# A two-matrix MLP by seven products: the sums of w_ff2 from DMA to VectorE, differences to GpSimd, and a last LayerNorm shared out

## The chip, the cores and the metric

One Trainium2 chip, one of its cores. The metric is the device time of one execution in microseconds (us), the median of several; smaller is better. Engines: PE is TensorE, DVE is VectorE, ACT is ScalarE, POOL is GpSimd, SP is SyncE (here it only issues DMAs).

## The reference

One layer of a hybrid encoder on 1024 frames of width 1024 (16 learned tokens are put in front and dropped at the end). The part that matters here is its second half:

```python
h  = layer_norm(ALPHA * h + mix, ln_mix_g, ln_mix_b)      # mix = concat(...) @ w_out
ff = square(relu(h @ w_ff1)) @ w_ff2                      # 1024 -> 4096 -> 1024
h  = layer_norm(ALPHA * h + ff, ln_ff_g, ln_ff_b)
```

All of it is float32.

## The kernel before

A float32 operand is split into a high part (a cast on ACT, line 128) and a low part (what is left, a subtraction on DVE, line 129); a product is three matmuls: high by high, high by low, low by high. `part` does this for an operand of 128x1024 and puts it into one of five `ring` slots (tile `hl`); a slot comes free when the product that read it has ended.

The first 560 us (LayerNorm, input projection, convolutions, attention, most of the output projection) are the same in both kernels. Then come:

- **The last projection tiles.** `mix_tile` (line 727) makes one 128-row tile of the residual stream `acc`; its LayerNorm has small statistics steps on GpSimd (lines 738 to 747 and `rsqrt`, lines 91 and 93) and two 128x1024 passes on DVE (lines 122 and 124). The tiles come in the order 6, 7, 4, 5, 0, 1, 2, 3.
- **x1**, the normalised stream turned by the TensorE (`x1_block`: four 128x128 transposes into PSUM, split into high and low). The MLP's two matrix products are done by Strassen and Winograd's seven products in place of eight, over 2x2 blocks, so sums and differences of blocks are needed as well: `xb21`, `xb11`, `xb22` are blocks, `xt2`, `xt3`, `xt4`, `xt1` are turned differences of them, made in `x1_t2`, `second_half` and `third_half` with `vsum` (line 811, DVE).
- **Eight groups** (`group(g)`, g = 0 to 7), each for 512 of the 4096 hidden columns. `first_product` makes seven products of 24 matmuls of 512 columns for h @ w_ff1 (line 885), with squared ReLU behind them (`relu2`, lines 906 to 908, tiles `relu`). Then `group` makes seven products for w_ff2 (line 894), each added into `acc` by `add_to` (line 1008). Group 0 makes x1 as it goes; the others load x1 back from DRAM.

The seven right operands made of w_ff2's 2x2 blocks (256x512 each, 128x1024 in SBUF, 512 KB) are, in the order of the products, b11, t3 = b22 + b12, t2 = t3 + b11, t3 again with b11 and b21 added (called T4 in the change), b11 + b12, b21 and b22. In the kernel before these sums are made **by DMA**: `w2_load` (SP's queue, line 990) puts a block into a tile and `w2_add` (GpSimd's queue, line 997) adds another block to it from DRAM while it lands. Six such additions run per group, on GpSimd's queue in the order t3, t2, t2, b11, t3, t3. The last two wait until the first form of t3 has been split, and each waits for the one before:

```python
b_, a_ = part(t3, 2), part(a21, 2)     # line 1070
w2_add(t3, g, 0, 0)                    # line 1071
w2_add(t3, g, 1, 0)                    # line 1072
...
b, a = part(t3, 2), part(a22, 2)       # line 1088, fourth product
```

Each engine does its instructions in program order, and the order on each is set by a scheduler when the kernel is built; an instruction that waits holds all behind it on the same engine. Each DMA queue is issued in order too.

**The end.** `finish_rows(t)` is the last LayerNorm of tile t: mean on DVE (line 1032), sum of squares on ACT (1035), (a - mean) times gain on DVE with the gain in PSUM (1036), rsqrt on GpSimd. For t >= 4 ACT then scales (1042), a GpSimd DMA adds the bias row (1043) and SP stores (1044); for t < 4 two DVE passes do it (1047), and SP or ACT's queue stores (1050, 1052). In the last group tiles 4 to 7 are finished before tile 0's last products.

## Time and profile before

| what | value |
|---|---|
| time, three runs | 1268.98, 1258.01, 1263.7 us; median 1263.7 |
| the profiled execution's own time | 1269.01 us |
| its span, first to last instruction | 1267.2 us (1.8 us lie outside) |
| mean granted TensorE clock | 0.968 of full speed |
| busy share of the span | PE 92%, PE weight load 78%, DVE 75%, ACT 44%, POOL 11% |
| the eight groups with the last LayerNorm | from about 585 us to the end |

Busy shares are means over stages. What ends last in a stage is read from the idle time ahead of an instruction and what released it, which stands in square brackets behind a row of the timeline.

### The profile page before, as it was taken

What the parts mean: (1) busy time and instruction counts of PE and PEld (TensorE: products, weight loads), DVE (VectorE), ACT (ScalarE), POOL (GpSimd) and SP (SyncE); (2) the same over time, 40 slices, a digit from 0 to 9 for tenths busy, and PEclk for the clock granted to TensorE, in tenths of its full rate; (3) what the DMA queues carried; (4) which work ended last, traced back from release to release, by engine and by line L of the source; (5) the groups of instructions that cost most, each with busy time, mean ns of one, the idle gap of its engine ahead of it and who ended that gap; (6) DMA issues with size and microseconds to landing.
All of it is one profiled execution on the core that took longest, in us unless ns stands there. A gap on an engine that the chain in (4) does not pass through costs nothing.

```text
span 1267.2 us, 15601 instructions
## 1 busy us (share of the span) xinstructions
PE 1163.5 (92%) x5982; PEld 992.7 (78%) x5982; DVE 949.6 (75%) x1179; ACT 560.5 (44%) x951; POOL 143.4 (11%) x259
## 2 busy tenths in 40 slices
PE   5999996899899798997999989999999999998993
PEld 5999995789798677885778878788788787886882
DVE  6799977978788699779678575684765946658477
ACT  4522115666566445433643423434334352343544
POOL 3300002010000100142110010010100101001003
PEclk9999997999999899998999989999999998999997
DMA  9313111021111612206966757657776676765436
GB/s 291 120 41 88 55 51 51 17 51 34 26 26 51 199 34 67 84 17 236 279 210 193 257 136 233 184 127 269 202 237 192 149 258 192 222 205 121 150 83 199
DMA packets 72458, 178.58 MB, mean 141 GB/s; under 512 B 3849, under 2 KB 27696, under 8 KB 68288
## 3 DMA queue, kind: packets, MB, share of 16 engines
q1 hardware_dynamic: 54528, 140.32, 30.9%
q0 software_dynamic: 15936, 31.46, 14.8%
q10 hardware_dynamic: 1920, 5.81, 1.3%
q8 instruction: 47, 0.77, 0.3%
q14 instruction: 27, 0.22, 0.1%
HBM read 152.41 MB, written 18.87 MB: 135 GB/s over the span
## 4 chain that ended last, share of the span: by engine, by line
PE 44%; DVE 14%; DMA 12%; issue 7%; ACT 5%; POOL 1%; DVEq 0%; ACTq 0%; POOLq 0%
PE ps_g L885 15%; PE ps_g L894 13%; DMA t<-in_w_ff_dram 11%; PE ps_g L210 6%; PE ps_g L630 4%; DVE keepp L463 3%; DVE hl L129 2%; PE ps_t L513 2%; DVE relu L906 1%; PE ps_g L455 1%; DMA y_raw<-yscr 1%; PE ps_o L486 1%; DVE beta L465 1%; PE ps_o L489 1%; ACT hl L128 1%
## 5 line engine op out<-in xcount | busy, mean ns | idle before, releaser
L894 PE MATMUL ps_g<-hl 128*128 128x512 f32 x1344 | 323.7, 401 | 19.7 <-ACT hl L128 15.3
L894 PEld LDWEIGHTS ps_g<-hl 128*128 128x128 f32 x1344 | 258.3, 194 | 83.9 <-ACT hl L128 22.7
L210 PE MATMUL ps_g<-xh,w_hl 128*128 128x346 f32 (+4 forms) x1024 | 258.7, 332 | 0.9 <-ACT beta L460 0.9
L210 PEld LDWEIGHTS ps_g<-xh,w_hl 128*128 128x128 f32 x1024 | 179.9, 192 | 9.6 <-ACT beta L460 1.1
L210 PE MATMUL ps_g<-xl,w_hl 128*128 128x346 f32 (+4 forms) x512 | 169.8, 332 | 0.8 <-DVE xl L129 0.8
L1008 DVE TENSOR_TENSOR acc<-acc,ps_g 128x1024 f32<-128x1024 f32 x96 | 116.3, 1215 | 28.1 <-PE ps_g L894 28.1
L885 PE MATMUL ps_g<-x_T,hl 128*128 128x512 f32 x576 | 133.5, 390 | 0.7 <-DVE hl L129 0.4
L885 PEld LDWEIGHTS ps_g<-x_T,hl 128*128 128x128 f32 x576 | 107.6, 188 | 24.4 <-DVE hl L129 0.8
L210 PEld LDWEIGHTS ps_g<-xl,w_hl 128*128 128x128 f32 x512 | 98.2, 192 | 5.0 <-DVE xl L129 1.1
L463 DVE TENSOR_TENSOR_SCAN keepp<-keepp 128x912 f32<-128x912 f32 (+7 forms) x64 | 87.6, 1380 | 11.9 <-ACT keepp L459 11.4
L885 PE MATMUL ps_g<-x_Y,hl 128*128 128x512 f32 x384 | 90.5, 390 | 1.8 <-ACT x_Y L128 1.2
L128 ACT CAST hl<-w_raw 128x1024 fp32r<-128x1024 f32 x55 | 56.1, 1049 | 76.5 <-DVE w_raw L811 76.5
L885 PEld LDWEIGHTS ps_g<-x_Y,hl 128*128 128x128 f32 x384 | 71.8, 188 | 17.7 <-ACT x_Y L128 1.5
L885 PE MATMUL ps_g<-x_X,hl 128*128 128x512 f32 x360 | 84.3, 389 | 0.0
L128 ACT CAST hl<-relu 128x1024 fp32r<-128x1024 f32 x48 | 50.4, 1050 | 74.8 <-PE ps_g L894 41.7
L129 DVE TENSOR_TENSOR hl<-w_raw,hl 128x1024 fp32r<-128x1024 f32 x55 | 65.7, 1220 | 23.5 <-ACT hl L128 23.5
L285 DVE SCALAR_TENSOR_TENSOR cacc<-glu,prm,cacc 128x482 f32<-128x482 f32 (+3 forms) x120 | 82.7, 743 | 0.3
L885 PEld LDWEIGHTS ps_g<-x_X,hl 128*128 128x128 f32 x360 | 67.5, 188 | 14.0
L455 PE MATMUL ps_g<-ks,q_hl 128*128 128x456 f32 (+8 forms) x224 | 59.0, 366 | 10.8 <-ACT beta L460 3.9
L906 DVE TENSOR_TENSOR relu<-ps_g,relu 128x1024 f32<-128x1024 f32 (+1 forms) x27 | 29.8, 1104 | 51.5 <-PE ps_g L885 51.5
L459 ACT ACTIVATE keepp<-ps_g 128x456 f32<-128x456 f32 (+8 forms) x112 | 51.9, 468 | 33.9 <-PE ps_g L455 16.1
L630 PE MATMUL ps_g<-w_hl,y 128*128 128x512 f32 x240 | 63.8, 402 | 1.9 <-DVE w_hl L129 1.8
(210 smaller groups left out, 1763.0 us busy)
## 6 DMA issues: line engine op xcount, KB each, us to landing
x_X<-xscr SPq DMA_DIRECT2D x14, 2048.0 KB, 7.8
x_Y<-xscr SPq DMA_DIRECT2D x14, 2048.0 KB, 10.4
w_raw<-in_w_ff_dram SPq DMA_DIRECT2D x16, 1024.0 KB, 10.4
t<-in_w_ff_dram POOLq DMA_DIRECT2D x24, 512.0 KB, 6.6
w<-in_w_ff_dram SPq DMA_DIRECT2D x24, 512.0 KB, 5.7
raw<-in_w_in_dram SPq DMA_DIRECT2D x22, 512.0 KB, 4.2
w<-in_w_ff_dram POOLq DMA_DIRECT2D x16, 512.0 KB, 5.9
xt<-in_x_dram SPq DMA_DIRECT2D x8, 512.0 KB, 5.8
```

Source lines behind the costliest of these rows:

```text
L128: nc.scalar.copy(out=h, in_=src)
L129: nc.vector.tensor_tensor(out=l, in0=src, in1=f32(h), op=ALU.subtract)
L210: nc.tensor.matmul(dst[:, :cw], lhsT=w[:, a, k, :], rhs=b[:, k, c0:c0 + cw], start=(i == 0), stop=(i == 3 * KT - 1))
L285: nc.vector.scalar_tensor_tensor(out=acc, in0=glu[j][:, o + k:o + k + n], scalar=prm[:, j, k:k + 1], in1=acc, op0=ALU.mult, op1=ALU.add)
L455: nc.tensor.matmul(zp[:, :cm], lhsT=qs[h][:, m, i * P:(i + 1) * P], rhs=ks[:, h, c0:c0 + cm], start=(m == 0), stop=(m == 1 and not last))
L459: nc.scalar.activation(out=kp[h][:, c0:c0 + cw], in_=zp[:, :cw], func=AF.Sigmoid, scale=-0.125)
L463: nc.vector.tensor_tensor_scan(out=rev, data0=rev, data1=rev, initial=1.0, op0=ALU.mult, op1=ALU.bypass)
L630: nc.tensor.matmul(dst, lhsT=y[a][:, t * P:(t + 1) * P], rhs=w[b][:, n * 512:(n + 1) * 512], start=(i == 0), stop=(i == last))
L885: nc.tensor.matmul(bk, lhsT=a[:, u, k, j * P:(j + 1) * P], rhs=x[:, v, k, :], start=(start and i == 0), stop=(i == 11), skip_group_check=True)
L894: nc.tensor.matmul(prs[tt // 2][:, tt % 2], lhsT=a[:, x, u, tt * P:(tt + 1) * P], rhs=b[:, y, u, :], start=(start and i == 0), stop=(i == ...
L906: nc.vector.tensor_tensor(out=r[:, j], in0=bk, in1=r[:, j], op=ALU.add)
L1008: nc.vector.tensor_tensor(out=a, in0=a, in1=prs[h], op=op)
```

## The change

- `group(g)` loads the four blocks b11, b21, b22, b12 of w_ff2 as four plain loads on SP's queue at its start, ahead of the first seven products. After the second product's operands DVE makes three sums of 128x1024: t3 = b22 + b12, t2 = t3 + b11, T4 = t2 + b21 (signs are kept in the left operands). One addition by DMA is left per group, b12 to b11 (line 998 of the changed kernel). b21 and b22 are loaded again for the last two products as before.
- In the last products of a group the difference a21 - a12 is made ahead of the fifth product instead of ahead of the seventh.
- In group 0, ten of twelve 128x512 differences for x1 (all but tile 3's, and all four in `third_half`) and three sums of w_ff1 blocks (128x1024) go from DVE to GpSimd (`gsum`).
- The first eight blocks of x1 (`x1_first`, four tiles) stand in the code ahead of the last projection tiles, and all four `x1_t2` in `second_half`.
- The first piece of w_ff1 (`early_part(0)`) is asked for ahead of the groups.
- Last LayerNorm: tiles 6 and 7 have (a - mean) times rsqrt on ACT, times gain on GpSimd, bias by GpSimd's DMA; tile 0 takes the way of tiles 4 and 5 (ACT, then the DMA for the bias).

```diff
+    def gsum(dst, a, b, op):
+        nc.gpsimd.tensor_tensor(out=dst, in0=a, in1=b, op=op)
+
     def x1_t2(t):
         x, y = acc[:, t], acc[:, 4 + t]
-        vsum(diffs[:, 0, t], x[:, HALF[1]], x[:, HALF[0]], ALU.subtract)
-        vsum(diffs[:, 1, t], diffs[:, 0, t], y[:, HALF[0]], ALU.add)
+        fsum = vsum if t == order[7] else gsum
+        fsum(diffs[:, 0, t], x[:, HALF[1]], x[:, HALF[0]], ALU.subtract)
+        fsum(diffs[:, 1, t], diffs[:, 0, t], y[:, HALF[0]], ALU.add)
         x1_block(xt2, diffs[:, 1, t], cols_of(t), True)
 
-    done = 0
+    for i in range(4):
+        x1_first(i)
     for i in range(FIRST, 8):
         run(mix_tiles(i, i + 1))
-        while done < min(4 + i - FIRST, 2 * (i - FIRST + 1)):
...
             relu2(c11, pa, 1.0)
-            vsum(a11, a11, a21, ALU.add)
+            gsum(a11, a11, a21, ALU.add)
             b = part(a11, 4)
-            vsum(a11, a11, a22, ALU.add)
+            gsum(a11, a11, a22, ALU.add)
             a = part(a11, 4)
             xt3 = second_half()
+            yield
             product1(a, xt2, pa, False)
             keep_sum(c21, pa)
-            vsum(a21, a21, a22, ALU.add)
+            gsum(a21, a21, a22, ALU.add)
...
+        if t >= 6:
+            rsqrt(rs[:, 0:1], sm[:, 2:3], P, 1, 1.0 / D, LN_EPS)
+            nc.gpsimd.tensor_tensor(out=rs[:, 1:2], in0=mean, in1=rs[:, 0:1], op=ALU.mult)
+            nc.scalar.activation(out=y, in_=a, func=AF.Identity, scale=rs[:, 0:1], bias=rs[:, 1:2])
+            nc.gpsimd.tensor_tensor(out=a, in0=y, in1=rows[0], op=ALU.mult)
+        else:
...
+        if t == 0 or t >= 4:
+            if t < 6:
+                nc.scalar.activation(out=a, in_=y, func=AF.Copy, scale=rs[:, 0:1])
+            nc.gpsimd.dma_start(out=a, in_=rows[1], accum_op=ALU.add)
+            nc.sync.dma_start(out=out_rows, in_=a)
             return
...
     def group(g):
         first, last = g == 0, g == NG - 1
+        b11, b21 = (raw_tile(n).rearrange("p (u c) -> p u c", u=2) for n in ("b11", "b21"))
+        b12, b22 = w2_tile(), w2_tile()
+        for t, (r, c) in ((b11, (0, 0)), (b21, (1, 0)), (b22, (1, 1)), (b12, (0, 1))):
+            w2_load(t, g, r, c)
         steps = first_product(g)
+        next(steps)
+        vsum(b22, b22, b12, ALU.add)
+        vsum(b12, b22, b11, ALU.add)
+        vsum(b21, b12, b21, ALU.add)
+        t3, t2, t4 = b22, b12, b21
         r0, r1 = next(steps)
-        b11, t3 = (raw_tile(n).rearrange("p (u c) -> p u c", u=2) for n in ("b11", "t3"))
-        t2 = w2_tile()
-        for t, (r, c) in ((t3, (1, 1)), (b11, (0, 0)), (t2, (1, 1))):
-            w2_load(t, g, r, c)
-        w2_add(t3, g, 0, 1)
-        w2_add(t2, g, 0, 1)
-        w2_add(t2, g, 0, 0)
...
         b_, a_ = part(t3, 2), part(a21, 2)
-        w2_add(t3, g, 0, 0)
-        w2_add(t3, g, 1, 0)
...
-        b, a = part(t3, 2), part(a22, 2)
+        b, a = part(t4, 2), part(a22, 2)
         product(a, b, pb, False)
         add_to(1, 0, pb, False, sums)
         b21, b22 = (w2_load(w2_tile(), g, 1, c) for c in range(2))
         b, a = part(b11, 2), part(a11, 2)
+        vsum(a21, a21, a12, ALU.subtract)
         product(a, b, pa, False)
...
-        vsum(a12, a21, a12, ALU.subtract)
...
             d = diffs[:, 1, t]
-            vsum(d, d, acc[:, 4 + t, HALF[1]], ALU.subtract)
+            gsum(d, d, acc[:, 4 + t, HALF[1]], ALU.subtract)
```

The order on DVE at the turn from group 2 to group 3, in the kernel before. `w_7340` is group 2's last block of w_ff2, `relu_6967` holds the left operand of its last product, `w_raw` is group 3's piece of w_ff1, `acc` rows are the additions of products.

```order
L1008 TENSOR_TENSOR acc<-acc,ps_g 128x2x512 x2
L129 TENSOR_TENSOR hl<-relu_6967,hl 128x1024
L129 TENSOR_TENSOR hl<-w_7340,hl 128x1024
L1008 TENSOR_TENSOR acc<-acc,ps_g 128x2x512
L811 TENSOR_TENSOR relu_6967<-relu_6968,relu_6967 128x2x512
L1008 TENSOR_TENSOR acc<-acc,ps_g 128x2x512
L129 TENSOR_TENSOR hl<-relu_6967,hl 128x1024
L1008 TENSOR_TENSOR acc<-acc,ps_g 128x2x512
L129 TENSOR_TENSOR hl<-w_raw,hl 128x1024
```

The same place in the changed kernel. `w_7443` and `w_7444` are group 3's blocks b12 and b22, in the buffers from which group 2's last two blocks (`w_7338`, `w_7340`) were split just before; `b_7441` is its b11, `b_7442` its b21.

```order
L129 TENSOR_TENSOR hl<-relu_6975,hl 128x1024
L129 TENSOR_TENSOR hl<-w_7340,hl 128x1024
L1009 TENSOR_TENSOR acc<-acc,ps_g 128x2x512 x2
L811 TENSOR_TENSOR w_7444<-w_7444,w_7443 128x1024
L129 TENSOR_TENSOR hl<-relu_6976,hl 128x1024
L129 TENSOR_TENSOR hl<-w_raw,hl 128x1024
L811 TENSOR_TENSOR w_7443<-w_7444,b_7441 128x1024
L1009 TENSOR_TENSOR acc<-acc,ps_g 128x2x512
L811 TENSOR_TENSOR w_raw<-w_raw 128x4x256
L1009 TENSOR_TENSOR acc<-acc,ps_g 128x2x512
L811 TENSOR_TENSOR b_7442<-w_7443,b_7442 128x1024
L811 TENSOR_TENSOR w_raw<-w_raw 128x4x256
```

The first sum of group 3's w_ff2 blocks now stands ahead of the split of group 2's last left operand (`relu_6976`), the other two among group 2's last additions; the difference of left operands has gone from here to an earlier place.

The order on GpSimd at the last two projection tiles (2 and 3), in the kernel before. `mv` and `rs` are their means and inverse deviations, `rms` a factor of the projection, `t_6212` a tile of w_ff2's sums.

```order
L997 DMA t_6212<-in_w_ff_dram 128x2x512
L91 TENSOR_SCALAR ve<-ssum_5626 128x2
L91 TENSOR_SCALAR ve<-rs 128x1
L93 TENSOR_TENSOR rms<-ve,mhalf 128x2
L93 TENSOR_TENSOR rs<-ve,mhalf 128x1
L738 TENSOR_TENSOR mv<-sm_5711 128x1
```

The same place in the changed kernel, from tile 2's mean to its inverse deviation. `x_T_5640` holds the differences, `w_raw` the first whole pieces of w_ff1.

```order
L738 TENSOR_TENSOR mv<-sm_5739 128x1
L739 TENSOR_SCALAR mv<-mv 128x1
L822 TENSOR_TENSOR x_T_5640<-acc 128x512
...
L822 TENSOR_TENSOR x_T_5640<-x_T_5640,acc 128x512
L738 TENSOR_TENSOR mv<-sm_5781 128x1
L822 TENSOR_TENSOR w_raw<-w_raw 128x4x256
L91 TENSOR_SCALAR ve<-rs 128x1
L739 TENSOR_SCALAR mv<-mv 128x1
L822 TENSOR_TENSOR w_raw<-w_raw 128x4x256
L93 TENSOR_TENSOR rs<-ve,mhalf 128x1
```

The DMA issue ahead of `rms` is gone, and four differences and two sums of w_ff1 now stand between tile 2's mean and its inverse deviation.

## Rows read from the trace of the kernel before

**Rows 1.** The page: the span, and busy time of PE.
```profile
span 1267.2 us, 15601 instructions
...
PE 1163.5 (92%) x5982; PEld 992.7 (78%) x5982; DVE 949.6 (75%) x1179; ACT 560.5 (44%) x951; POOL 143.4 (11%) x259
```
**Rows 2.** Windows: stretch, length, busy (count) PE, PEld, DVE, ACT, POOL; PEclk, DMA, GB/s.
```profile
681.41:764.55 83.14, 79.73 (x337) 64.86 (x336) 54.31 (x47) 32.03 (x32) 7.15 (x6) 0.96 0.69 201
764.55:847.27 82.72, 79.79 (x338) 64.84 (x336) 53.92 (x47) 32.02 (x32) 7.15 (x6) 0.96 0.66 196
847.27:926.11 78.84, 77.03 (x337) 62.91 (x336) 53.68 (x47) 32.03 (x32) 7.17 (x6) 1.00 0.67 203
926.11:1004.18 78.07, 77.04 (x337) 62.91 (x336) 53.69 (x47) 32.04 (x32) 7.16 (x6) 1.00 0.70 210
1004.18:1086.42 82.24, 79.53 (x337) 64.70 (x336) 53.86 (x47) 32.03 (x32) 7.15 (x6) 0.96 0.68 201
1086.42:1168.72 82.30, 78.54 (x337) 63.90 (x336) 53.86 (x47) 32.05 (x32) 7.15 (x6) 0.98 0.66 198
570.00:605.00 35.00, 26.14 (x124) 19.62 (x122) 32.78 (x47) 15.29 (x27) 8.83 (x18) 0.85 0.69 240
```
**Rows 3.** Timeline of PE, groups 0 to 5: start, length, what, count, [idle before <-releaser].
```profile
681.41 5.60 PE L885 MATMUL ps_g<-x_X,hl 128*128 128x512 f32 x24
686.85 5.60 PE L885 MATMUL ps_g<-x_Y,hl 128*128 128x512 f32 x24
...
822.04 25.39 PE L894 MATMUL ps_g<-hl 128*128 128x512 f32 x96 [2.93 <-ACT hl L128]
...
980.83 1.20 PE L894 MATMUL ps_g<-hl 128*128 128x512 f32 x4 [0.15 <-ACT hl L128]
```
**Rows 4.** The chain that ended last, group 2's second half: start, length, what.
```profile
800.32 13.29 DMA t<-in_w_ff_dram
...
813.90 6.08 DMA t<-in_w_ff_dram
```
**Rows 5.** Timeline of DVE in group 4's last two products.
```profile
991.20 1.22 DVE L129 TENSOR_TENSOR hl<-w,hl 128x1024 fp32r<-128x1024 f32 x1
...
995.88 1.23 DVE L129 TENSOR_TENSOR hl<-relu,hl 128x1024 fp32r<-128x1024 f32 x1
```
**Rows 6.** DMA issues: what, queue, count, KB each, median us to landing; then line 990's spread.
```profile
w<-in_w_ff_dram SPq DMA_DIRECT2D x24, 512.0 KB, 5.7
t<-in_w_ff_dram SPq DMA_DIRECT2D x8, 512.0 KB, 3.5
...
DMA to landing us min/median/max: 3.5/4.7/9.2
```
**Rows 7.** Timeline: a GpSimd step of one column, alone and beside DVE.
```profile
551.64 0.19 POOL L738 TENSOR_TENSOR mv<-sm 128x1 f32<-128x1 f32 x1 [2.09 <-DVE acc L734]
...
573.32 1.28 DVE L124 SCALAR_TENSOR_TENSOR acc<-acc,rs,norm 128x1024 f32<-128x1024 f32 x1
573.48 1.17 POOL L738 TENSOR_TENSOR mv<-sm 128x1 f32<-128x1 f32 x1 [1.03 <-DVE acc L734]
```
**Rows 8.** Groups of GpSimd's instructions by form: busy us, mean ns.
```profile
L566 POOL MEMSET ac<- 128x1024 f32 x1 | 1.0, 951 | 0.0
...
L571 POOL TENSOR_SCALAR_AFFINE_SELECT past<-past 128x128 f32<-128x128 f32 x1 | 0.3, 283 | 0.0
```
**Rows 9.** Timeline, last projection tiles and group 0's third product.
```profile
569.32 1.28 POOL L997 DMA_DIRECT2D t<-in_w_ff_dram  x1 [2.15 <-DVE ssum L696]
...
571.97 0.75 DVE L734 SCALAR_TENSOR_TENSOR acc<-ps_g,rms,acc 128x512 f32<-128x512 f32 x1 [2.95 <-POOL rms L93]
...
605.34 4.83 PE L885 MATMUL ps_g<-x_T,hl 128*128 128x512 f32 x20 [0.40 <-DVE hl L129]
```
**Rows 10.** Timeline of the end: PE's last products, and a store on SP's queue.
```profile
1237.00 0.70 PE L894 MATMUL ps_g<-hl 128*128 128x512 f32 x2 [1.48 <-DVE acc L1013]
...
1258.61 0.33 SPq L1044 DMA_DIRECT2D out_dram<-acc  x1
```

More of the change, by code (lines that the diff above doesn't have):

```diff
@@ L819, in x1_first @@
         x1_block(xb11, acc[:, t, HALF[0]], cols_of(t))
+    def gsum(dst, a, b, op):
+        nc.gpsimd.tensor_tensor(out=dst, in0=a, in1=b, op=op)
     def x1_t2(t):
         x, y = acc[:, t], acc[:, 4 + t]
-        vsum(diffs[:, 0, t], x[:, HALF[1]], x[:, HALF[0]], ALU.subtract)
-        vsum(diffs[:, 1, t], diffs[:, 0, t], y[:, HALF[0]], ALU.add)
+        fsum = vsum if t == order[7] else gsum
+        fsum(diffs[:, 0, t], x[:, HALF[1]], x[:, HALF[0]], ALU.subtract)
+        fsum(diffs[:, 1, t], diffs[:, 0, t], y[:, HALF[0]], ALU.add)
         x1_block(xt2, diffs[:, 1, t], cols_of(t), True)
-    done = 0
+    for i in range(4):
+        x1_first(i)
     for i in range(FIRST, 8):
         run(mix_tiles(i, i + 1))
-        while done < min(4 + i - FIRST, 2 * (i - FIRST + 1)):
-            if done < 4:
-                x1_first(done)
-            else:
-                x1_t2(order[done])
-            done += 1
     x = acc[:, order[7], :]
@@ L923, in first_product @@
             pa = pair(0)
-            product1(early_part(0), xb11, pa, True)
+            product1(early[1], xb11, pa, True)
             a11, a21, a12, a22 = w1_load(0)
             relu2(c11, pa, 1.0)
-            vsum(a11, a11, a21, ALU.add)
+            gsum(a11, a11, a21, ALU.add)
             b = part(a11, 4)
-            vsum(a11, a11, a22, ALU.add)
+            gsum(a11, a11, a22, ALU.add)
             a = part(a11, 4)
             xt3 = second_half()
+            yield
             product1(a, xt2, pa, False)
             keep_sum(c21, pa)
-            vsum(a21, a21, a22, ALU.add)
+            gsum(a21, a21, a22, ALU.add)
             pb = pair(0)
@@ L963, in first_product @@
             a = part(a11, 4)
+            yield
             product1(a, xt2, pa, False)
@@ L1024, in ln_ff_rows, with finish_rows @@
         nc.scalar.activation(out=bk.rearrange("p h c -> p (h c)"), in_=rows[0], func=AF.Copy, scale=ROOT_D)
-        return rows[1], bk
-    def finish_rows(t, sm, fb, gps):
+        return rows, bk
+    def finish_rows(t, sm, rows, gps):
         a = acc[:, t, :]
@@ L1035, in finish_rows @@
         nc.scalar.activation(out=y2[:, 1], in_=a, func=AF.Square, bias=mean, accum_out=sm[:, 2:3])
-        nc.vector.scalar_tensor_tensor(out=y.rearrange("p (h c) -> p h c", h=2), in0=a.rearrange("p (h c) -> p h c", h=2),
-                                       scalar=mean, in1=gps, op0=ALU.add, op1=ALU.mult)
         rs = small([P, 2], "rs")
-        rsqrt(rs[:, 0:1], sm[:, 2:3], P, 1, 1.0, D * LN_EPS)
-        rows = slice(t * P, (t + 1) * P)
-        if t >= 4:
-            nc.scalar.activation(out=a, in_=y, func=AF.Copy, scale=rs[:, 0:1])
-            nc.gpsimd.dma_start(out=a, in_=fb, accum_op=ALU.add)
-            nc.sync.dma_start(out=os_[rows, :], in_=a)
+        out_rows = os_[t * P:(t + 1) * P, :]
+        if t >= 6:
[4 more added lines that the diff above has]
+        else:
+            nc.vector.scalar_tensor_tensor(out=y.rearrange("p (h c) -> p h c", h=2), in0=a.rearrange("p (h c) -> p h c", h=2),
+                                           scalar=mean, in1=gps, op0=ALU.add, op1=ALU.mult)
+            rsqrt(rs[:, 0:1], sm[:, 2:3], P, 1, 1.0, D * LN_EPS)
+        if t == 0 or t >= 4:
[3 more added lines that the diff above has]
+            nc.sync.dma_start(out=out_rows, in_=a)
             return
         for n in range(2):
-            nc.vector.scalar_tensor_tensor(out=a[:, HALF[n]], in0=y[:, HALF[n]], scalar=rs[:, 0:1], in1=fb[:, HALF[n]],
+            nc.vector.scalar_tensor_tensor(out=a[:, HALF[n]], in0=y[:, HALF[n]], scalar=rs[:, 0:1], in1=rows[1][:, HALF[n]],
                                            op0=ALU.mult, op1=ALU.add)
             if t == 3:
-                (nc.sync, nc.scalar)[n].dma_start(out=os_[rows, HALF[n]], in_=a[:, HALF[n]])
+                (nc.sync, nc.scalar)[n].dma_start(out=out_rows[:, HALF[n]], in_=a[:, HALF[n]])
         if t < 3:
-            nc.sync.dma_start(out=os_[rows, :], in_=a)
+            nc.sync.dma_start(out=out_rows, in_=a)
     def group(g):
@@ L1100, in group @@
             add_to(0, 0, pc, False)
-            b, a = part(b22, 2), part(a12, 2)
+            b, a = part(b22, 2), part(a21, 2)
             product(a, b, pa, False)
@@ L1104, in group @@
             return
-        b_, a_ = part(b22, 2), part(a12, 2)
+        b_, a_ = part(b22, 2), part(a21, 2)
         ln = ln_ff_rows()
@@ L1124, in second_half @@
     def second_half():
-        x1_t2(order[6])
-        x1_t2(order[7])
+        for t in order[4:]:
+            x1_t2(t)
         xt3 = x_tile(x1p, "X")
@@ L1167, in hybrid_layer @@
     ffp = pool("ffp", side="left")
+    early.append(early_part(0))
     for g in range(NG):
```

## The prediction

> **What bounds the kernel now.** I read the page's busy times first, then the chain that ended last, then PE's timeline from one group to the next, and last the stretches at both ends of the MLP. PE is busy for 92% of the span [rows 1], so what can be won is PE's idle time and the time in which it runs at a lower clock. The timeline of PE shows both. Two products of 24 matmuls start 5.44 us apart (686.85 - 681.41) [rows 3], so a group of 14 products needs 14 x 5.44 = 76.2 us. From the first product of one group to that of the next, groups 1 to 6 take 83.14, 82.72, 78.84, 78.07, 82.24 and 82.30 us [rows 2]: 487.3 in all where 6 x 76.16 = 457.0 would do. The excess is 30.3 us.
>
> The reader is to see where it lies. In each group PE stops once, ahead of the fourth w_ff2 product, for 2.93 us in group 2 but only 0.15 us in group 4, both times until ACT's cast of an operand [rows 3]. The chain shows behind that cast two DMAs in a row into tile t, of 13.29 and 6.08 us [rows 4]: the second form of t3, to which two blocks are added by DMA, one after the other. The rest is the clock: in group 2 the 96 matmuls behind the stop took 25.39 us [rows 3] where 4 x 5.44 = 21.8 would do, and the stretches with a long stop were granted 0.96 to 0.98 of full speed, those with a short one 1.00 [rows 2], so PE ran part of the time at the lower of its two levels, 1.2 in place of 2.4 GHz, after it had stood still. A stop thus costs about twice its length.
>
> **Term 1, the sums of w_ff2 in groups 1 to 6.** The change takes five of six added DMAs away and gives DVE three sums of 128x1024; one sum of that shape takes as long as a split, 1.22 us [rows 5], so 3.7 us a group. DVE is busy for 53.7 us in such a stretch [rows 2]; with 57.4 of 76.2 us it has room. The four plain loads are issued when the buffers come free at the end of the group before, more than 40 us ahead of the product that stopped; its operand then only waits for a ring slot, as the others do. So the stop goes: -30.3 us.
>
> What is late next: the first of the new sums stands on DVE ahead of the split of the old group's last left operand (front, the two orders of DVE), and it needs two loads that can only be issued when that group's last block of w_ff2 has been split, since they take its buffers. In group 4 that split starts at 991.20 and the last left operand's at 995.88 [rows 5]. A 512 KB load lands 3.5 us after its issue when it is alone; the median of those into the w tiles is 5.7 and the longest of line 990 is 9.2 [rows 6]. Two together, taken as 5.1 to 5.7: the loads are there at 991.20 + 1.22 + 5.1 to 5.7 = 997.5 to 998.1, the sum ends 1.22 later, the split 1.22 after that, at 999.9 to 1000.5. The last product starts 5.44 us ahead of the next group, at 1004.18 - 5.44 = 998.7, and wants the low part from its third matmul, at 999.2. That is 0.7 to 1.3 us late. In group 4 this split itself came a little late behind the remains of the stop, so I take 0.7: 6 x 0.7 = +4.2. Bounds: nothing, where the loads land in 3.5; with 9.2 it is 4.8 us late, and the clock may fall behind it. Queued behind the waiting sum are the next group's first splits, with 5.44 us more to spare. Term 1: -26.1 (bounds -30 to -12, with 3 us left per group).
>
> **Term 2, group 0's first half.** From 570 to 605 us DVE is busy for 32.78 of 35 us [rows 2] and PE waits for it; group 0's third product gets going at 605.34, after a DVE split [rows 9]. The change takes from DVE in this stretch ten differences of 128x512 (half of a 1.22 us pass plus its start, some 0.65 each) and three sums of 1.22: about 10 us; it adds up to 3.7 us of w_ff2 sums. It also takes away the DMA issue of 1.28 us on GpSimd, behind which rms was late and DVE idle for 2.95 us [rows 9]. Against this GpSimd gets ten differences and three sums. No row shows its price for two inputs. A fill of 128x1024 takes 0.95; a pass with one input of 128x128 takes 0.283, eight of them 2.26 [rows 8]. I take 2.0 for 1024 columns and 1.0 for 512, nearer the upper row because two inputs are read: 10 x 1.0 + 3 x 2.0 = 16 us. And the small steps of tiles 2 and 3, on which their LayerNorm waits, now stand behind these on GpSimd (front, the orders of GpSimd).
>
> GpSimd and DVE don't run side by side freely: a step of 0.19 us took 1.17 beside a DVE pass with two inputs in SBUF, and ended just after it [rows 7]. The Trainium skill says of this ("SBUF — State Buffer", Who interferes with whom) that a DVE instruction with two SBUF inputs and a GpSimd one that reads SBUF exclude each other, whichever began first, for a whole instruction; the row agrees for GpSimd's wait, and no run here yet shows DVE waiting for GpSimd.
>
> I walk the new order from 573, when tile 2's mean can start. On GpSimd four differences and two sums (8 us) stand ahead of tile 2's rs, then four differences (4 us) ahead of tile 3's. Behind tile 3's rs DVE has its LayerNorm pass (1.28), two differences, two additions of 512 columns and two splits of that size (6 x 0.65), and five passes of 1.22 ahead of the third product's last operand: 11.3 us, with a semaphore or two 12. If the engines don't hold each other, tile 3's rs is there some 15 us on with the small steps, at 588 to 590, and the product goes at about 602. If each pair excludes the other, GpSimd also waits for some six passes of DVE of 1.28 ahead of that rs, at 596, and DVE for two of GpSimd's behind it (3 us): about 611. Transposes that stood before this product now stand in it, but they have to be done anyway. I take 608, a little on the second side, so +3. Bounds -3 and +9, since a PE that stands still for long also runs slower behind it.
>
> **Term 3, the last group and the end.** The difference of left operands no longer stands among the last additions, where PE waited 1.48 us for DVE [rows 10]: -1.2, one pass of DVE. Then DVE loses two passes with gain and two with bias, about 4 us. But tiles 0 and 7 now end by a GpSimd DMA, and the last such before let SP's store wait until 1258.61 [rows 10]; in the changed order tile 7's comes later on GpSimd, behind a 2 us multiplication and tile 0's DMA, and stores of tiles 2 and 3 stand behind it on SP. The DMA then sets the end in DVE's place: -1 (bounds -4 and +3).
>
> Everything ahead of 560 us stands in the same order and is counted at nothing.
>
> **Sum.** -26.1 + 3 - 1.2 - 1 = -25.3. The profiled execution took 1269.0 us (1267.2 of span and 1.8 outside), so 1243.7. It lies 5.3 us above the median of the runs, 1263.7; the stops vary most (0.15 to 2.93 us), so I take it that quicker runs had shorter ones and have less to win. From the median, the whole sum would give 1238.4; I say 1242.
>
> **The rivals.**
> *GpSimd's price.* Each of its passes blocks DVE, and the steps of tiles 2 and 3 come late: term 2 is +9, the tail with its multiplication +2, term 1 -24. Sum -24 + 9 - 1.2 + 2 = -14, time 1254 from the middle between profiled time and median (less 1 to 2). For it: rows 7 and the order of GpSimd. Against it: most of what DVE does there reads PSUM. The rule named above is this rival's.
> *The stop has a second cause.* Group 4's stop was 0.15 us and its stretch still took 78.07, 1.9 over [rows 2, 3]; if that part comes from ring slots, it stays: 6 x 1.9 = 11.4 of the 30.3. Term 1 is -19 less 2, sum about -17, time 1250. Against it: the splits behind the late operand are themselves pushed together by it.
> *The cover holds everywhere.* Loads land in 3.5 us, GpSimd works beside DVE: -30 - 3 - 1.2 - 4 = -38, time 1229.
> *Slower.* The new sum at the group's turn is the new stop. Its place is DVE's queue ahead of the last left operand's split; the price is 4.8 us a group with loads of 9.2 us, and 3 more by the clock, 7.8 against the 5.05 that go: 6 x 2.75 = +16, with term 2 at +5 and the rest at nothing +21, time 1286. It decides from loads that take some 7.5 us on, where its stop with the clock passes 5 us a group. Against it: at that time SP's queue has little else in flight.
> *The change doesn't do what it says*: a sum that the scheduler put late. The order shows all three ahead of the next group's second product, so only the first can hurt; this is in the case above.
>
> **How the numbers follow.** Forecast 0.52 (1234 to 1249), GpSimd's price 0.15, second cause 0.11, cover everywhere 0.17, slower 0.05. The range reaches to 1227 (most of the better case) and to 1259 (over the first two rivals); it leaves out the slower case and half of the best. A measurement of this kernel can tell about 1% from no change, 12.6 us: below 1251 is faster. The forecast, the better case and most of the second cause, with a little of GpSimd's price, lie there: 0.79; the rest of the two, and some that is lost on both, 0.16; slower 0.05.
>
> **What would show it.** In the changed profile groups 1 to 6 should take 76.2 to 78 us each with a granted clock of 1.00; no DMA stands in the chain there; DVE waits once per group for DMA at the first new sum, less than 3 us. In group 0 the third product starts between 602 and 611, and GpSimd's passes of 128x512 take about 1 us alone, 128x1024 about 2; DVE's passes with two SBUF inputs would be seen longer than 1.3 us if they are held. The end from PE's last matmul to the last store is as long as before or 1 to 3 us shorter. I am wrong if the stop ahead of the fourth w_ff2 product is still there, if a new one of over 2 us stands ahead of the seventh, or if group 0 gives back more than 10 us.

## The result and the profile after

The changed kernel takes 1246.0 us (median of four runs, 1245.3 to 1247.3) where the kernel before takes 1263.0 beside it: a ratio of 0.9865, 95% interval 0.9821 to 0.9909. The forecast was 1242. The profiled executions differ by more, 1269.0 to 1245.3, and what follows is told of these two. In which stretch the quicker executions of before were shorter isn't known, since only one of each kernel is profiled.

The page of the kernel after, span and busy times, answers to [rows 1]:

```profile
span 1243.5 us, 15574 instructions
...
PE 1150.7 (93%) x5982; PEld 990.6 (80%) x5982; DVE 969.6 (78%) x1186; ACT 563.1 (45%) x952; POOL 124.6 (10%) x237
```

PE lost 12.8 us of busy time with the same 5982 matmuls, so it ran less at its lower clock; DVE got 20 us more to do, and the kernel is faster all the same. The windows from the first product of one group to that of the next answer to [rows 2] (same columns; the last row is the stretch 570 to 605 us):

```profile
688.63:764.79 76.16, 76.16 (x338) 63.06 (x336) 56.92 (x50) 32.26 (x32) 1.21 (x1) 1.00 0.52 186
...
1069.43:1145.59 76.16, 76.16 (x338) 63.06 (x337) 56.94 (x50) 32.26 (x32) 1.18 (x1) 1.00 0.52 187
570.00:605.00 35.00, 23.44 (x104) 18.44 (x102) 28.51 (x32) 16.45 (x29) 29.34 (x25) 0.83 0.61 225
```

All six rows read 76.16, which is 14 x 5.44: PE does not stop once in groups 1 to 6, and its clock is 1.00. That is the full 30.3 us. In PE's timeline the seven w_ff2 products are one unbroken run of 168 matmuls where [rows 3] had a stop ahead of the fourth:

```profile
917.11 5.60 PE L884 MATMUL ps_g<-x_X,hl 128*128 128x512 f32 x24
...
955.19 38.24 PE L893 MATMUL ps_g<-hl 128*128 128x512 f32 x168
```

The next two fences answer to [rows 4 to 6]. The one wait that the new sums have, in DVE's timeline in the last two products of group 3 (the row after the sum is the split of the last left operand):

```profile
903.26 1.22 DVE L129 TENSOR_TENSOR hl<-w,hl 128x1024 fp32r<-128x1024 f32 x1
...
908.22 1.23 DVE L811 TENSOR_TENSOR w<-w,w 128x1024 f32<-128x1024 f32 x1 [0.57 <-DMA w<-in_w_ff_dram]
909.36 1.22 DVE L129 TENSOR_TENSOR hl<-relu,hl 128x1024 fp32r<-128x1024 f32 x1
```

and the DMA issues of w_ff2's blocks (queue, count, KB, median us to landing; the last row is the additions by DMA that stay):

```profile
w<-in_w_ff_dram SPq DMA_DIRECT2D x32, 512.0 KB, 6.4
...
b<-in_w_ff_dram SPq DMA_DIRECT2D x16, 512.0 KB, 3.6
...
b<-in_w_ff_dram POOLq DMA_DIRECT2D x8, 512.0 KB, 7.7
```

The last load is issued at 904.5, as soon as the split of 903.26 has read its buffer, and the sum starts 3.7 us later. The split of the last left operand ends at 910.6, and its product starts at 917.11 - 5.44 = 911.67: in time by a microsecond.

The gain of 30.3 is not what the span shows (23.7). To find the rest I count from a fixed point, DVE's last reduction of `ssum` (line 696): up to it both kernels run the same instructions, though it came at 568.87 in the profiled execution of before and at 567.98 in that of after. From there to group 1's first product it is 681.41 - 568.87 = 112.5 us before and 688.63 - 567.98 = 120.7 after. So group 0 gave back 8.1. From group 7's first product to the end it is 98.5 and 97.9. The account: -30.3 + 8.1 - 0.6, and -0.9 ahead of the point, is -23.7.

Where the 8.1 lie, GpSimd's timeline shows (answers to [rows 7 and 8]; `x_T` are differences of 128x512, `w_raw` W1 sums of 128x1024, `rs` with line 93 the step that tile 2's, then tile 3's last LayerNorm pass needs):

```profile
572.41 1.29 POOL L822 TENSOR_TENSOR x_T<-acc 128x512 f32<-128x512 f32 x1
...
578.78 2.40 POOL L822 TENSOR_TENSOR w_raw<-w_raw 128x1024 f32<-128x1024 f32 x1
...
584.04 0.55 POOL L93 TENSOR_TENSOR rs<-ve,mhalf 128x1 f32<-128x1 f32 x1
...
584.72 2.35 POOL L822 TENSOR_TENSOR x_T<-x_T,acc 128x512 f32<-128x512 f32 x1
587.02 1.17 POOL L747 TENSOR_TENSOR rs<-sm 128x1 f32<-128x1 f32 x1
588.15 2.27 POOL L822 TENSOR_TENSOR x_T<-acc 128x512 f32<-128x512 f32 x1
...
594.10 0.57 POOL L93 TENSOR_TENSOR rs<-ve,mhalf 128x1 f32<-128x1 f32 x1
```

and DVE's timeline beside it shows who waits (answers to [rows 9]):

```profile
585.83 2.32 DVE L122 SCALAR_TENSOR_TENSOR acc<-acc,mv,norm 128x1024 f32<-128x1024 f32 x1
...
594.70 3.38 DVE L124 SCALAR_TENSOR_TENSOR acc<-acc,rs,norm 128x1024 f32<-128x1024 f32 x1 [2.60 <-POOL rs L93]
```

In before the pass of line 124 for tile 3 is this one:

```profile
589.52 1.27 DVE L124 SCALAR_TENSOR_TENSOR acc<-acc,rs,norm 128x1024 f32<-128x1024 f32 x1
```

Read the lengths first. A difference takes 1.29 us alone and 2.27 to 2.35 beside a DVE pass with two inputs in SBUF; the DVE passes of lines 122 and 124, 1.28 alone [rows 7], take 2.32 and 3.38. Each engine waits for the other. Then read the order: ten such passes, with the small steps between them, stand ahead of tile 3's rs on GpSimd, and the LayerNorm pass that waits for it starts at 594.70, 26.7 us after the fixed point, where before it started at 589.52 - 568.87 = 20.7. The third product's main part starts at 610.88 in place of 605.34 [rows 9], from the fixed point 42.9 us in place of 36.5: 6.4 of the 8.1. Most of what comes on top by the fourth product is the clock. PE had stood still in several stretches ahead of that product and was granted 0.50 of full speed, its lower level of 1.2 GHz, from 605.0 to 610.8 and 0.72 on the mean from 610.8 to 616.4, where before had 1.00 from 603.7 to 617.0. The first seven matmuls of the main part take 3.1 us in place of 1.7.

At the end (answers to [rows 10]) a GpSimd multiplication, ACT behind it, and the last stores on SP's queue:

```profile
1219.34 2.42 POOL L1043 TENSOR_TENSOR acc<-y,ln_ff 128x1024 f32<-128x1024 f32 x1
...
1221.79 1.15 ACT L1036 ACTIVATE y<-acc,sums 128x1024 f32<-128x1024 f32 x1 [1.42 <-POOL acc L1043]
...
1228.35 1.15 POOL L1051 DMA_DIRECT2D acc<-ln_ff  x1
...
1236.06 0.33 SPq L1052 DMA_DIRECT2D out_dram<-acc  x1
1236.49 1.04 SPq L1060 DMA_DIRECT2D out_dram<-acc  x1
1237.62 1.15 SPq L1058 DMA_DIRECT2D out_dram<-acc  x1
```

ACT's square waits for the multiplication, since tile `y` has two buffers; and the store of a tile closed by an added DMA (issued 1228.35, stored 1236.06) holds the stores behind it on SP. The added DMA ahead of that one, issued 0.8 us before it, landed at 1232.34, and this one 3.7 us later.

### The profile page after: what moved, and what is told of

It reads as the page before. It is cut to its first block, busy times and chain, and to the rows that moved or that the text cites. A ratio compares the mean times of both kernels' runs of the same rounds, so it can differ in the third digit from the quotient of the medians.

```text
span 1243.5 us, 15574 instructions
## 1 busy us (share of the span) xinstructions
PE 1150.7 (93%) x5982; PEld 990.6 (80%) x5982; DVE 969.6 (78%) x1186; ACT 563.1 (45%) x952; POOL 124.6 (10%) x237
## 4 chain that ended last, share of the span: by engine, by line
PE 64%; DVE 8%; ACT 3%; POOL 3%; issue 2%; DMA 2%; DVEq 0%; ACTq 0%; POOLq 0%
PE ps_g L884 24%; PE ps_g L893 24%; PE ps_g L210 6%; PE ps_g L630 4%; DVE keepp L463 3%; PE ps_t L513 2%; PE ps_g L455 1%; DMA y_raw<-yscr 1%; PE ps_o L486 1%; PE ps_o L489 1%; DVE beta L465 1%; POOL x_T L822 1%; ACT keepp L459 1%; DVE al L129 1%; DMA q_hl<-q_hl 1%
## 5 line engine op out<-in xcount | busy, mean ns | idle before, releaser
L893 PE MATMUL ps_g<-hl 128*128 128x512 f32 x1344 | 306.5, 389 | 2.3 <-DVE hl L129 1.6
L893 PEld LDWEIGHTS ps_g<-hl 128*128 128x128 f32 x1344 | 252.0, 188 | 55.6 <-DVE hl L129 2.0
L884 PEld LDWEIGHTS ps_g<-x_Y,hl 128*128 128x128 f32 x384 | 72.9, 191 | 19.6 <-DVE hl L129 2.6
L129 DVE TENSOR_TENSOR hl<-w_raw,hl 128x1024 fp32r<-128x1024 f32 x55 | 67.2, 1258 | 20.7 <-ACT hl L128 20.7
```

The costliest lines, as they stand in the source:

```text
L129: nc.vector.tensor_tensor(out=l, in0=src, in1=f32(h), op=ALU.subtract)
L884: nc.tensor.matmul(bk, lhsT=a[:, u, k, j * P:(j + 1) * P], rhs=x[:, v, k, :], start=(start and i == 0), stop=(i == 11), skip_group_check=True)
L893: nc.tensor.matmul(prs[tt // 2][:, tt % 2], lhsT=a[:, x, u, tt * P:(tt + 1) * P], rhs=b[:, y, u, :], start=(start and i == 0), stop=(i == ...
```

## The experiments

Each was run beside the kernel before, on the same chip as it. The table gives the profiled execution in the three stretches used above, each worked out from the timelines as told there, then the median of the runs and its ratio to before. Each ratio goes by the median of before that stood beside it (1263.0 in the first two rows, 1263.7 to 1265.6 in the others).

| kernel | fixed point to group 1 | one of groups 1 to 6 | group 7 to end | median us | ratio, 95% |
|---|---|---|---|---|---|
| before | 112.5 | 81.2 | 98.5 | 1263.0 | |
| after | 120.7 | 76.16 | 97.9 | 1246.0 | 0.982 to 0.991 |
| e1 all sums on VectorE | 117.5 | 76.16 | 97.9 | 1243.2 | 0.977 to 0.987 |
| e2 w_ff2 sums alone | 112.5 | 76.16 | 96.3 | 1235.4 | 0.971 to 0.981 |
| e3 without w_ff2 sums | 121.1 | 81.2 | 102.3 | 1278.5 | 1.006 to 1.016 |
| e5 T4's sum early | 120.0 | 79.2 | 97.6 | 1261.5 | 0.992 to 1.004 |
| e6 T4's sum late | 113.8 | 76.16 | 96.5 | 1237.7 | 0.976 to 0.985 |
| e8 differences on VectorE | 116.4 | 76.16 | 98.1 | 1240.9 | 0.979 to 0.987 |
| e8 W1 sums on VectorE | 113.5 | 76.16 | 98.0 | 1238.7 | 0.977 to 0.987 |
| e4 old end | 120.7 | 76.16 | 94.8 | 1242.4 | 0.980 to 0.988 |
| e11 GpSimd part of the end | 120.4 | 76.16 | 96.1 | 1244.6 | 0.981 to 0.987 |
| e12 DMA part of the end | 120.6 | 76.16 | 97.4 | 1246.2 | 0.982 to 0.989 |
| e9 e2 + early difference | 112.9 | 76.16 | 94.3 | 1234.3 | 0.973 to 0.979 |
| e10 two parts undone | 113.5 | 76.16 | 94.6 | 1236.1 | 0.975 to 0.980 |

### What the w_ff2 sums bring (e2, e3, e5, e6)

**e2_ff2_only**: the kernel before with this part of the change, and with what places the sums: two `yield`s in `first_product`, and the first piece of w_ff1 asked for ahead of the groups as in the change.

```diff
-        w2_add(t3, g, 0, 1)
-        w2_add(t2, g, 0, 1)
-        w2_add(t2, g, 0, 0)
...
-        w2_add(t3, g, 0, 0)
-        w2_add(t3, g, 1, 0)
...
+        vsum(b22, b22, b12, ALU.add)
+        vsum(b12, b22, b11, ALU.add)
+        vsum(b21, b12, b21, ALU.add)
```

> The kernel before, with the w_ff2 sums of the change alone (four plain loads, three sums on VectorE, T1 by an added DMA); the differences, the order of the x1 blocks and the end are those of before. Theory: groups 1 to 6 take 76.2 us each, group 0 is 0 to 4 us later than before (three sums of 1.22 more on VectorE), the end is as before; the time is 4 to 8 us under the changed kernel's, 1238 to 1242. Rival (the w_ff2 sums themselves are what delays group 0): the first product of group 1 starts at 688 or later, the time is 1245 to 1250.

Measured: 1235.4 us, below what the theory gave; group 0 is as before to 0.04 us. DVE's wait for rms, 2.95 us in [rows 9], is 1.37 here, as GpSimd's DMA issue ahead of it is gone. The three new sums of 1.2 us cost group 0 nothing on balance; that the shorter wait pays for them is read, not tried. This part alone beats the whole change by 10 us.

**e3_no_ff2**: the changed kernel with w_ff2's sums by DMA again; the other parts alone.

> The changed kernel with the w_ff2 sums by DMA as before: the GpSimd differences, the new order and the new end alone. Theory: groups 1 to 6 take what they took before (78 to 83 us each), group 0 is 4 to 8 us later than before, the end 0 to 1 us shorter; the time is 3 to 8 us above the kernel before, some 1266 to 1271. Rival (the w_ff2 sums delay group 0): the time equals that of before within 2 us, and the first product of group 1 starts at 681 to 683.

Measured: 1278.5, 1.1% slower than before, more than the theory gave. Group 0 is 8.5 late; the end is 3.8 longer where I had expected it a little shorter. Taken together, the parts of the change other than the w_ff2 sums lose.

**e5_t4_alone** and **e6_t4_reload**: the kernel before, with only the two last of the six added DMAs replaced. In e5 the block comes by a load of its own, so the scheduler is free to put the sum early (upper half of the diff); in e6 it is loaded into t3 behind t3's split, so the sum can only come then (lower half).

```diff
-        w2_add(t3, g, 0, 0)
-        w2_add(t3, g, 1, 0)
+        vsum(b21, t2, b21, ALU.add)                               # e5
...
+        w2_load(t3, g, 1, 0); vsum(t3, t2, t3, ALU.add)           # e6
```

> The kernel before, with one sum alone changed: the two blocks that were added by DMA to t3 after its first split are gone, T4 is T2 plus a block that a plain load brings, in one sum on VectorE. Three added DMAs a group stay (one to t3, two to t2), and the one to b11. Theory (the stop came from the two chained DMAs that can only start behind t3's first split): groups 1 to 6 take 76.2 to 77 us each, the time is 24 to 30 us under the profiled time of before, 1236 to 1245. Rival (any added DMA among the w_ff2 blocks stops PE, the chain only most often): the groups keep half of their excess, 78 to 81 us each, and the time is 1248 to 1256.

Measured: 79.2 us a group, which is within the rival's 78 to 81, and 1261.5 in all, which is above both. The stop is another one: that ahead of the fourth product is gone, and one stands where the next group begins. Timelines of DVE and PE in e5 at the end of group 1 (`w_raw` is the next group's W1 sum):

```profile
766.50 1.23 DVE L811 TENSOR_TENSOR w<-w,w 128x1024 f32<-128x1024 f32 x1 [6.04 <-DMA w<-in_w_ff_dram]
...
767.64 1.21 DVE L1008 TENSOR_TENSOR acc<-acc,ps_g 128x1024 f32<-128x1024 f32 x1
768.77 1.22 DVE L811 TENSOR_TENSOR w_raw<-w_raw 128x1024 f32<-128x1024 f32 x1
...
768.95 5.70 PE L885 MATMUL ps_g<-x_X,hl 128*128 128x512 f32 x24 [1.38 <-issue]
```

The sum stands early on DVE and waits 6.04 us for T2's two added DMAs. The addition behind it, which reads a product out of PSUM, comes late, and PE with it: PE starts the next group 0.10 us after that addition has ended (768.85), and so it does at each of the seven turns. A group still takes 3.1 us too long (79.24 - 76.16). This is the rival of my prediction by which a new sum is the new stop, made real by a sum that waits for a chain of DMAs and not for one load, and by way of an addition, not of the last left operand's split.

> The kernel before, with one thing changed: behind t3's first split one plain load of the last block into t3 and one sum with T2 on VectorE take the place of the two chained added DMAs. The other three added DMAs of a group stay. Theory (PE stopped because these two DMAs, 13.3 and 6.1 us, had to fit between t3's split and the fourth product): the load lands within 6 us, groups 1 to 6 take 76.2 to 77.0 us each, the time is 1235 to 1242. Rival (any wait of VectorE on a DMA, or the added DMAs that stay, keeps a stop): 78 to 82 us a group, 1248 to 1262.

Measured: 1237.7, groups at 76.16, and the chain of that stretch is PE alone:

```profile
759.91 36.04 PE ps_g L885 x159
795.95 38.08 PE ps_g L894 x168
834.03 6.12 PE ps_g L885 x27
```

So the stop came from the two chained additions by DMA behind t3's split. The other four added DMAs of a group are still there, and the new load too can only start behind that split; one plain load and one sum in place of the two are enough.

### What group 0 gives back (e1, e8)

**e1_vector_sums**: the changed kernel, `gsum` calling VectorE (13 sums back).

> The changed kernel, with the ten differences of 128x512 and the three sums of 128x1024 of group 0 on VectorE again; all else stays. Theory (GpSimd's long passes, which hold VectorE and keep the rs steps of tiles 2 and 3 waiting, are what group 0 gives back): the first product of group 1 starts at 680 to 684 us in place of 688.6, tile 3's rs comes some 5 us earlier than 594, groups 1 to 6 stay at 76.2 us each, and the time is 1238 to 1242. Rival (group 0 is late because VectorE now also has the three w_ff2 sums, and because of the new order of the x1 blocks): VectorE then has some 10 us more to do, and the start stays at 688 or comes later, the time is 1246 to 1254.

Measured: 117.5, between the two. 3.2 of the 8.1 us go, 4.9 stay. DVE's timeline says why they stay. In e1 it does, in this order:

```profile
601.12 1.23 DVE L811 TENSOR_TENSOR w<-w,w 128x1024 f32<-128x1024 f32 x1 [0.60 <-DMA w<-in_w_ff_dram]
...
602.86 1.22 DVE L811 TENSOR_TENSOR w_raw<-w_raw 128x1024 f32<-128x1024 f32 x1
604.00 1.22 DVE L129 TENSOR_TENSOR hl<-w_raw,hl 128x1024 fp32r<-128x1024 f32 x1
```

and in e2, with the same sums on the same engine:

```profile
597.12 1.21 DVE L811 TENSOR_TENSOR w_raw<-w_raw 128x1024 f32<-128x1024 f32 x1
...
598.85 1.21 DVE L129 TENSOR_TENSOR hl<-w_raw,hl 128x1024 fp32r<-128x1024 f32 x1
599.98 1.21 DVE L811 TENSOR_TENSOR w<-w,w 128x1024 f32<-128x1024 f32 x1
```

In e1 the scheduler put a w_ff2 sum, for a product that starts after 646, ahead of the W1 sum and the split for which PE waits in the third product (`hl<-w_raw`, at 605). PE's timelines show what comes of it, in e1 and then in e2:

```profile
605.27 6.45 PE L884 MATMUL ps_g<-x_T,hl 128*128 128x512 f32 x20 [1.53 <-DVE hl L129]
```

```profile
600.11 4.83 PE L885 MATMUL ps_g<-x_T,hl 128*128 128x512 f32 x20 [0.40 <-DVE hl L129]
```

From the fixed point this is 38.0 us in e1 and 35.5 in e2, so 2.5 of the 4.9 are there by then. The same 20 matmuls then take 1.6 us longer, at a granted clock of 0.76 (605 to 612) in place of 1.00. That the order is the cause of all this is read, not tried.

**e8_diffs_vector** puts the six differences ahead of the third product back on VectorE and leaves the rest; **e8_w1_vector** does so with the three W1 sums.

```diff
-        fsum = vsum if t == order[7] else gsum
+        fsum = vsum                                               # e8_diffs_vector
...
-            gsum(a11, a11, a21, ALU.add)
+            vsum(a11, a11, a21, ALU.add)                          # e8_w1_vector, and the other two
```

> The changed kernel with the six differences ahead of the third product on VectorE; the three W1 sums and the four later differences stay on GpSimd. Times from the last rms reduction (0) of that run, where the changed kernel has tile 3's last LayerNorm pass at 26.7, group 1 at 120.7. Theory (GpSimd's queue ahead of the rs steps): rs of tile 3 stands behind one or two W1 sums of 2.4 us only, the pass comes at 20 to 23, group 1 starts at 113 to 117, the time is 1239 to 1243. Rival (the order of the x1 blocks costs the time, whoever sums): group 1 at 117 to 121, 1243 to 1247.

> The changed kernel with the three W1 sums of group 0 on VectorE; all ten differences stay on GpSimd. Same zero as in the run with the differences on VectorE. Theory (queue and hold): four differences of 1.3 us stand ahead of tile 2's rs and none ahead of tile 3's, the pass comes at 20 to 23, group 1 starts at 114 to 118, the time is 1240 to 1244. Rival (the order of the x1 blocks): group 1 at 117 to 121, 1243 to 1247.

Measured: 116.4 with the differences back; 113.5 with the W1 sums back, better than its theory and 1.0 from before. In both, tile 3's LayerNorm pass starts 19.6 and 19.8 us after the fixed point where after has 26.7. GpSimd's timeline of the second (W1 sums on VectorE) shows tile 3's step with no long pass ahead of it, and DVE's pass behind it:

```profile
581.37 0.24 POOL L747 TENSOR_TENSOR rs<-sm 128x1 f32<-128x1 f32 x1 [0.96 <-ACT squares L744]
581.69 0.19 POOL L91 TENSOR_SCALAR ve<-rs 128x1 f32<-128x1 f32 x1
581.97 0.55 POOL L93 TENSOR_TENSOR rs<-ve,mhalf 128x1 f32<-128x1 f32 x1
...
587.21 1.73 DVE L124 SCALAR_TENSOR_TENSOR acc<-acc,rs,norm 128x1024 f32<-128x1024 f32 x1
```

In the first the pass is early too, but W1 sums and DVE hold each other:

```profile
578.24 3.15 DVE L122 SCALAR_TENSOR_TENSOR acc<-acc,mv,norm 128x1024 f32<-128x1024 f32 x1
...
581.95 2.87 POOL L822 TENSOR_TENSOR w_raw<-w_raw 128x1024 f32<-128x1024 f32 x1
```

So both halves of the theory stand: the row of passes ahead of rs, and the holding. Against e2 the differences alone cost 1.0, the W1 sums (with the four later differences) 3.9, both together 8.1. They don't add up: only together do they push tile 3's rs out to 26 us. Against e1, which has the changed kernel's order of blocks and nothing of this on GpSimd, each alone even gains: 3.9 us (117.5 to 113.5) with the differences on GpSimd, 1.1 (to 116.4) with the W1 sums and the four later differences. Both together cost 3.2 (to 120.6). So it isn't the move to GpSimd as such that loses here, but so much of it ahead of the steps of tiles 2 and 3; the scheduler's order differs a little in each of the four, which these numbers include.

### What the end gives back (e4, e11, e12)

**e4_old_end**: the changed kernel with `finish_rows` of before. **e11_end_gps** keeps of the new end only the ScalarE and GpSimd passes of tiles 6 and 7, **e12_end_dma** only the added DMA of tile 0.

```diff
-        if t == 0 or t >= 4:
+        if t >= 4:                                                # e11, in the changed kernel
...
-        if t >= 4:
+        if t == 0 or t >= 4:                                      # e12, in e4
```

> The changed kernel with the last LayerNorm of before (every row's centre and gain pass on VectorE, tiles 4 to 7 closed by an added DMA, tiles 0 to 3 by VectorE). Theory (the new end gives back what it takes: its GpSimd multiplications and DMA issues stand ahead of the rs steps of tiles 1 to 3): from the first product of group 7 to the end of the span 95.5 to 96.8 us in place of 97.9, as the run with the w_ff2 sums alone had 96.3; the time is 1244 to 1245. Rival (the new end gains the 1 us that was forecast for it): 98 to 99.5 us, the time is 1246.5 to 1248.

> The changed kernel, with tile 0 closed by VectorE as before; tiles 6 and 7 keep their ScalarE and GpSimd passes. Theory (GpSimd's two multiplications of 2.4 us hold one of the two y buffers, for which ScalarE's squares wait, and the rs steps behind them): 97.0 to 98.2 us from group 7's first product to the end of the span. Rival (tile 0's added DMA and its store, ahead of those of tiles 1 to 3, are what costs): 94.5 to 95.8.

> The changed kernel, with the last LayerNorm of tiles 6 and 7 as before; tile 0 keeps its ScalarE pass and its added DMA. Theory (GpSimd's multiplications cost the 3 us): 94.3 to 95.5 us from group 7's first product to the end of the span. Rival (tile 0's added DMA costs them): 96.8 to 98.2.

Measured: e4 has 94.8, so the new end costs 3.2, more than its theory. e11 has 96.1, between its theory and its rival, and e12 97.4, its rival's value: GpSimd's part alone costs 1.4 us (96.13 - 94.75), the added DMA alone 2.6 (97.40 - 94.75), and both together 3.2, not 4.0. The larger one is tile 0's added DMA, against my theory. In e12 DVE's last pass ends at about 1235.9, but SP:

```profile
1237.77 0.33 SPq L1045 DMA_DIRECT2D out_dram<-acc  x1
1238.19 1.21 SPq L1053 DMA_DIRECT2D out_dram<-acc  x1
1239.49 1.18 SPq L1051 DMA_DIRECT2D out_dram<-acc  x1
```

issues its last store only at 1239.49, since tile 0's store (1237.77) waited there for a DMA issued at 1228.99. The last three of these DMAs are issued at 1222.44, 1225.68 and 1228.99 and land at 1229.97, 1234.05 and 1237.75, about 4 us apart: a fifth one lands behind the fourth. In e4, where DVE's last pass ends at about 1235.1, the same last store stands directly beside it:

```profile
1231.81 0.33 SPq L1045 DMA_DIRECT2D out_dram<-acc  x1
1232.23 2.19 SPq L1053 DMA_DIRECT2D out_dram<-acc  x2
1234.52 1.19 SPq L1051 DMA_DIRECT2D out_dram<-acc  x1
```

### Versions that beat both (e9, e10)

**e9_early_left** is e2 with the change's earlier difference of left operands; **e10_w1_vector_old_end** is the changed kernel with the W1 sums on VectorE and the old end.

```diff
+        vsum(a21, a21, a12, ALU.subtract)      # e9: ahead of the product, into a21
         product(a, b, pa, False)
...
-        vsum(a12, a21, a12, ALU.subtract)
```

> The kernel before with the w_ff2 sums of the change and its earlier difference of left operands; x1's differences, block order and last LayerNorm as before. Theory (these two parts are all that gains): 112 to 113.5 us from the last rms reduction to group 1, 76.16 us for each of groups 1 to 6, 94.5 to 95.2 from group 7's first product to the end of the span (the run with the w_ff2 sums alone had 96.3); the time is 1231 to 1235, below the changed kernel by 11 to 15. Rival (the earlier difference only moves the wait): 96 to 97 at the end, the time is 1235 to 1237.

> The changed kernel with two parts undone: the three W1 sums of group 0 on VectorE, and the last LayerNorm of before. The ten differences stay on GpSimd. Theory (the parts add up): 113 to 114 us from the last rms reduction to group 1, 94.5 to 95.2 from group 7's first product to the end; the time is 1233 to 1237. Rival (they don't add up, since what one gives back was hidden by the other): 1237 to 1241.

Measured: 1234.3 and 1236.1, both stretches within 0.2 us of what their theories had. The earlier difference takes 2.0 us off the end (96.3 to 94.3), but not by PE, whose last matmul comes 0.65 us later than in e2 (79.86 and 79.21 from group 7's first product). It lies in the stores: in e2 a store waits on SP for its added DMA until 1221.20, and the last of the three behind it is issued 0.8 us after DVE's last pass; in e9 that wait ends 1.6 us earlier in the stretch, and the last store stands directly behind DVE. Why the DMA lands earlier isn't tried. Against before, e9 is at 0.9759 (0.9730 to 0.9788). Between e9, e2 (1235.4) and e10 the medians lie within 2 us, with ranges of 2 to 6 us each: which of the three is best isn't settled. That all three beat the change, by some 10 us, is: their intervals (up to 0.981) lie below that of the change (from 0.982).

## Why the prediction was right, and where it was off

The direction, its cause and the order of the terms held: 1246.0 measured for 1242, within the likeliest case's range. That the time is so close is in part luck: the three terms were off by -4.2, +5.1 and +1.6 us, which nearly cancel, so that the profiled executions differ by 23.7 where the sum was 25.3. That quicker executions of before have less to win was right: the medians differ by 17.0.

**Term 1** was said to be -26.1 and is -30.3. The step that failed is the new sum's wait for its load, +0.7 a group. I took two loads together, landing in 5.1 to 5.7 us. They are issued 5.4 us apart (899.1 and 904.5), the second lands in 3.6, and DVE waits 0.57. The bound "nothing, where the loads land in 3.5" was the right value, and the reading that a sum's wait for a DMA is the danger was right too: e5 has one that stops PE. The second rival (another cause of the stop) is refuted: nothing stayed of 78.07, each group takes 76.16. It rested on a misreading: 0.15 was only the first of group 4's stops. PE's timeline of before goes on, in the same fourth product:

```profile
982.72 0.50 PE L894 MATMUL ps_g<-hl 128*128 128x512 f32 x1 [0.69 <-ACT hl L128]
983.40 20.94 PE L894 MATMUL ps_g<-hl 128*128 128x512 f32 x91 [0.18 <-DVE hl L129]
```

Together that is 1.03 us, and the excess of 1.9 is about twice it, as in all six groups together (30.3 for 15.7 us of standing still). That the stop came from the two chained DMAs, e6 shows.

**Term 2** was said to be +3 and is +8.1, near its bound of +9. Three steps of the walk were off. GpSimd's prices: 1.28 and 2.40 where I took 1.0 and 2.0, about a fifth too little; 10 x 1.28 + 3 x 2.40 = 20.0, not 16 us. The holding: tile 3's rs came at 594.1, beside the walk's 596 for full exclusion and not its 588 to 590, and the third product's main part at 610.88, the walk's "about 611" (in the times of before, both 0.9 later). I had split the difference at 608, where the row on the step of 1.17 [rows 7] spoke for one side only. And the fourth product fell back by 2 us more, 1.4 of them in the third's first matmuls at the lower clock; the prediction had put that slower running into its upper bound only.

The Trainium skill has a rule for the holding ("SBUF — State Buffer", Who interferes with whom): two SBUF inputs on DVE and a GpSimd read of SBUF exclude each other for a whole instruction. The trace now agrees from both sides, GpSimd's 1.29 to 2.35 and DVE's 1.28 to 2.32 and 3.38. The Trainium skill also gives a price that I passed over ("GPSIMD Engine Reference", Elementwise — side-by-side cycle accounting): 4497 ns for a two-input pass of 2048 float32 columns, so by estimate 2.25 for 1024; the trace has 2.40.

**Term 3** was said to be -2.2 and is -0.6. The early difference gave -2.0 (forecast -1.2), but by luck: PE was to wait less for DVE, and it does not. In the changed kernel it still stands still there, four matmuls further on, for a split:

```profile
1215.00 8.91 PE L893 MATMUL ps_g<-hl 128*128 128x512 f32 x38 [1.59 <-DVE hl L129]
```

The gain of e9 lies in the stores, as told above. The w_ff2 sums gave another -2.2 in the last group (98.5 to 96.3 in e2), for which the sum had no term. It isn't the gain of the other groups once more, since before has no stop ahead of group 7's fourth product; among its last 42 matmuls PE waits 1.6 us in e2 where before has 3.1. The new end cost +3.2 where I said -1, past the upper bound of +3. It does relieve DVE: PE's last matmul comes 78.3 us after group 7's first product, 79.9 in e4. But the stretch behind it, forecast as long as before or 1 to 3 us shorter, takes 19.6 us (e4 14.9, before 16.5). That a DMA would set the end in DVE's place was right, but its landing (7.7 us from issue to store, 1228.35 to 1236.06, behind the DMA ahead of it) stood in no step of the sum. The three parts make -1.0, within 0.4 of the -0.6 measured.

The rival on GpSimd's price came near in its second and third terms (+9 and +2 said, +8.1 and, for the new end, +3.2 measured) and missed the first (-24). The better case had the first (-30) and missed the other two. Each is half of what happened.

## What to carry to other kernels

The sums made by added DMAs cost nothing here until two of them, chained, had to start behind a use of the same tile; so look for such a pair first, and replace it alone. Work that is moved to GpSimd "because it is idle" can be paid in three ways: by its own longer pass, by DVE passes that it holds, and by the small steps behind it on its queue. Here, in the changed kernel's order of blocks, either half alone was worth moving and both together were not (and the old order with neither, e2, was faster than all), so count what stands ahead of the small steps. And a store that waits for a slow DMA holds every store behind it on the same queue; issuing the slow one last or on a queue of its own would avoid that, which no run here tries.
